# Reordering the steps of two attention mixers in a two-layer decoder trunk on one NeuronCore

## Chip, core and metric

The kernel runs on one core of a Trainium2 chip. The metric is device time in microseconds (us) of one execution. Before the change the median of three runs is 2033.67 us (2032.64 to 2034.67).

## What is computed

The input is 512 positions of width 1024, float32. Each of two layers adds half a SwiGLU feed-forward (width 2816), a mixer, and half a SwiGLU again. The reference, cut to what matters:

```python
for layer in range(2):
    x = x + 0.5 * swiglu_half(x, ffn1...)
    h = rms_norm(x, mix_norm[layer])
    if layer == 0:
        z = h @ ab_w_in
        mixed = concat([mla_mixer(z[..., :416], ...), dilated_mixer(z[..., 416:], ...)]) @ ab_w_out
    else:
        z = h @ cd_w_in
        mixed = concat([swa_mixer(z[..., :768], ...), nsa_mixer(z[..., 768:], ...)]) @ cd_w_out
    x = x + mixed
    x = x + 0.5 * swiglu_half(x, ffn2...)
```

`mla_mixer` projects to a latent, expands it to 8 heads of queries and keys, norms them, rotates a part and attends causally. `dilated_mixer` has three groups of 4 heads with bands at distances 1, 4 and 16, merged by their log-sum-exp. `swa_mixer` is banded attention with sinks (window 128, 8 query heads, 2 key heads). `nsa_mixer` adds compressed, selected and windowed attention under gates (8 query heads, 2 key heads).

## The kernel before

Every product of float32 matrices is made from three matmuls (`TERMS`): each operand is split into a high and a low float32r part (`split`, L164: ScalarE copies the high part, VectorE subtracts), and high x high, high x low and low x high are summed in PSUM. Weights stream from HBM through three `raw` buffers on SyncE's queue, and are split as they come (`weight`, L131). Activations lie transposed, 8 tiles of 128 x 512 (`xh`, `xl`).

`build` runs feed-forward, `mix0`, feed-forward, feed-forward, `mix1`, feed-forward. Each feed-forward is 1584 matmuls of 512 columns.

A mixer is a list of steps. `emit` (L111) walks a string (`ORDER0`, L42, or `ORDER1`, L47); each word names a step, and the digits are its arguments. The steps are recorded in that order, and the order sets their priority; a word with `!` is recorded with the priority of the mixer's start, so a scheduler in the build places it as early as its inputs and buffers let it. The scheduler then fixes one order for each engine, and at run time each engine takes its instructions strictly in that order, waiting at any whose input isn't there. PSUM has 8 banks by use: two for scores (`s`), two for transposes (`t`), one for an attention output (`o`), one for transposes of queries and keys (`q`), two for products (`f`).

The steps of the first mixer (`mix0`, L594):

- `a10`, `a00`, `a20`: projection of queries and keys of a dilated group (`proj`, L386: 96 matmuls of 512 columns, out `pz`), then `head_norm` (L409) on VectorE. `a01`, `a11`, `a21`: transposes of the normed result (`pt<-zqk`). `a12`, `a02`: projection of values (96 matmuls, of 512 and of 256 columns).
- `p0`, `p1`: `latent_prep` (L762) of four latent heads each: 36 matmuls (out `pq`, `pk`), squares, a chain of small VectorE operations (`rsq`, `rsqrt`), and scaling to `lq`, `lk` (L806, L807).
- `h0` to `h3`: `latent_pair` (L810), two heads of causal attention: transposes of queries and keys (`pqt<-lq`, `pqt<-lk`), scores (`s<-qt`), reduction and exponential (`scores`, L447), scaling by the row sums (`scale_rows`, L475), transposes of the weights (`pt<-e`), products with the values (`po`). `h0`, `h1` need `p0`; `h2`, `h3` need `p1`.
- `s10` and the other `s`: scores of a dilated group for a pair of heads (`s<-qkt`). `o0`, `o1`: their merge, transposes and products.

After the list, `out_projs` (L564) multiplies the features by the output weights (out `py`): 48 matmuls with the features of `h0` and `h1`, then 96 with the others.

The second mixer (`mix1`, L834) has `c`, `q0`, `q1`, `n`, `v`, `u0`, `u1`: projections of 96 matmuls of 256 columns (`part`, L839; `q` the queries of the sparse attention, `u` the banded queries, each for one key head and followed by `head_norm`); `C`: compression; `S0`, `S1`, `W0`, `W1`: splits (`stack`, L986) and transposes (`stack_t`, L993, `pqt<-qst`) of the normed queries, for the sparse (`S`) and the banded (`W`) attention; `D0`, `D1`: compressed attention; `s00`, `s01`, `s10`, `s11`: two heads each of selected and full-window attention (`selected`, L1034, scores `s<-kth,qst`); `w00` to `w11`: two heads each of banded attention (`window`, L1054).

Of the kernel before, what the change touches and what calls it, by code (L numbers as in the profile page):

```python
# [38 lines left out]
TERMS = ((0, 0), (1, 0), (0, 1))  # L39


ORDER0 = """a10 p0 a00 a20 a01 h0 !a11 a12 a02 !h1 p1 s10 h2 !s00 a21 s02 !s11 !s12 s01 h3 !o0 !o1"""  # L42

SCALE_F, SCALE_D, SCALE_T, SCALE_W = "vgvg", "gavv", "ggav", "avgv"
SQUARE = "ggva"
PARTS0 = [1, 0], [3, 4, 5, 2]
ORDER1 = """c q0 C n S0 q1 !v D0 s00 u0 !u1 W0 s01 w00 !S1 !W1 w01 !D1 s10 !w10 s11 w11"""  # L47
PARTS1 = [5, 4], [2, 6], [1, 0, 3, 7]


# [8 lines left out]
class Trunk:  # L59
# [534 lines left out]
    def mix0(self, nj):  # L594
# [29 lines left out]
        def turned(g):  # L624
# [9 lines left out]
        sc = [{}, {}]  # L634
        self.emit(ORDER0, {
            "a": lambda g, n: (queries_keys, turned, values)[n](g),
# [197 lines left out]
    def mix1(self, nj):  # L834
# [4 lines left out]
        def part(n, scaled=False):  # L839
            z = two([self.u("z", "zp") for _ in range(2)])  # L840
            self.proj(A["cd%d" % n], nat,
                      lambda i, p: nc.scalar.activation(z[i], p, AF.Copy, scale=r[:, i:i + 1] if scaled else 1.0))
            return z

        def heads(z):
            self.head_norm([t.rearrange("p (h e) -> p h e", h=4) for t in z], r=r)
            return z
# [34 lines left out]
        def kv():  # L882
# [3 lines left out]
        self.hold = None  # L886
        self.emit(ORDER1, {
            "q": lambda g: zq.update({g: heads(part((2, 6)[g]))}),
# [301 lines left out]
```

## Time and profile before

| what | value |
| --- | --- |
| runs | 2032.64, 2033.67, 2034.67 us |
| profiled execution, its own time | 2036.73 us |
| its span, first to last instruction | 2034.9 us |
| TensorE (PE) busy | 1991.1 us, 98% |
| VectorE (DVE) busy | 1012.5 us, 50% |
| ScalarE (ACT) busy | 756.0 us, 37% |
| GpSimd (POOL) busy | 159.2 us, 8% |
| mean granted TensorE clock | 0.988 of full |

Times inside the execution are microseconds from the span's start. A busy time of PE is a sum over what ran, and a matmul at a lower granted clock is longer, so PE can be busy all the time and still lose time to the clock. The first mixer lies at about 375 to 670, the second at about 1390 to 1670.

### The profile page before, as it was taken

Reading aid. Unit: us, or ns where it says so; the run is one execution under the profiler, and the core shown is the slowest. Engines: PE = TensorE matmul, PEld = TensorE weight load, DVE = VectorE, ACT = ScalarE, POOL = GpSimd, SP = SyncE. Lnnn points to the kernel's source line nnn. Section 1 sums busy time; section 2 is a strip of 40 time slices with the busy share of each in tenths; the row PEclk is TensorE's granted clock in tenths of the full one; section 3 lists DMA queues with packets and bytes.
Section 4 is the critical chain, followed back from the end, with each engine's and each line's share of the span. In section 5 each row is a group of like instructions: output and inputs, shape, how many; then the busy total and the mean of one; then the engine's idle time right before and its main releaser. Section 6 shows DMA issues by size and latency. Waiting matters only on the chain. (4 is left out here: it accounts for less than half of the span.)

```text
span 2034.9 us, 24712 instructions
## 1 busy us (share of the span) xinstructions
PE 1991.1 (98%) x9559; PEld 1639.8 (81%) x9559; DVE 1012.5 (50%) x1956; ACT 756.0 (37%) x1298; POOL 159.2 (8%) x219
## 2 busy tenths in 40 slices
PE   8999999999989999999999999999999999999999
PEld 6888888987857888888888888889976678888887
DVE  6443444474455644344454434444766666433442
ACT  4222333345546432223333223333367753322231
POOL 6000001011022100000100000011011120000000
PEclk9999999999979999999999999999999999999999
DMA  6523224431111322322332332244202032233223
GB/s 189 179 88 109 99 87 131 132 98 42 45 42 45 114 100 85 105 94 95 92 110 88 95 102 104 92 150 146 73 19 74 23 102 95 90 93 107 104 87 100
DMA packets 72853, 194.54 MB, mean 96 GB/s; under 512 B 9540, under 2 KB 16216, under 8 KB 72736
## 3 DMA queue, kind: packets, MB, share of 16 engines
q1 hardware_dynamic: 70752, 186.90, 27.9%
q0 software_dynamic: 1984, 6.06, 1.2%
q8 instruction: 75, 1.23, 0.3%
q14 instruction: 42, 0.34, 0.0%
HBM read 186.59 MB, written 12.35 MB: 98 GB/s over the span
## 5 line engine op out<-in xcount | busy, mean ns | idle before, releaser
L169 DVE TENSOR_TENSOR wlo<-raw,whi 128x1024 fp32r<-128x1024 f32 (+4 forms) x386 | 397.5, 1030 | 521.4 <-ACT whi L168 512.2
L168 ACT CAST whi<-raw 128x1024 fp32r<-128x1024 f32 (+4 forms) x386 | 345.3, 895 | 738.9 <-PE pu L162 298.9
L162 PE MATMUL pg<-xh,whi 128*128 128x512 f32 x704 | 276.1, 392 | 6.7 <-ACT xh L171 6.7
L162 PE MATMUL pg<-xl,whi 128*128 128x512 f32 x704 | 275.4, 391 | 1.5 <-DVE xl L172 1.5
L162 PE MATMUL pg<-xh,wlo 128*128 128x512 f32 x704 | 276.0, 392 | 0.0
L162 PE MATMUL pu<-xh,wlo 128*128 128x512 f32 x704 | 274.6, 390 | 0.0
L162 PE MATMUL pu<-xh,whi 128*128 128x512 f32 x704 | 274.3, 390 | 0.0
L162 PE MATMUL pu<-xl,whi 128*128 128x512 f32 x704 | 273.9, 389 | 0.0
L162 PE MATMUL py<-ah,whi 128*128 128x512 f32 x704 | 273.9, 389 | 0.0
L162 PE MATMUL py<-al,whi 128*128 128x512 f32 x704 | 273.9, 389 | 0.0
L162 PE MATMUL py<-ah,wlo 128*128 128x512 f32 x704 | 273.9, 389 | 0.0
L301 ACT ACTIVATE tg<-tg 128x512 f32<-128x512 f32 x88 | 55.6, 632 | 323.0 <-DVE tg L300 323.0
L162 PEld LDWEIGHTS pg<-xh,whi 128*128 128x128 f32 x704 | 132.7, 188 | 36.1 <-ACT xh L171 7.8
L162 PEld LDWEIGHTS pg<-xh,wlo 128*128 128x128 f32 x704 | 132.8, 189 | 34.7 <-DVE wlo L169 1.0
L162 PEld LDWEIGHTS pg<-xl,whi 128*128 128x128 f32 x704 | 132.6, 188 | 28.5 <-DVE xl L172 3.7
L162 PEld LDWEIGHTS pu<-xh,wlo 128*128 128x128 f32 x704 | 132.3, 188 | 27.6 <-issue 0.2
L162 PEld LDWEIGHTS pu<-xl,whi 128*128 128x128 f32 x704 | 132.1, 188 | 27.7 <-issue 0.2
L162 PEld LDWEIGHTS pu<-xh,whi 128*128 128x128 f32 x704 | 132.3, 188 | 27.4
L162 PEld LDWEIGHTS py<-al,whi 128*128 128x128 f32 x704 | 132.1, 188 | 27.5
L162 PEld LDWEIGHTS py<-ah,wlo 128*128 128x128 f32 x704 | 132.1, 188 | 27.4
L162 PEld LDWEIGHTS py<-ah,whi 128*128 128x128 f32 x704 | 132.1, 188 | 27.4
L300 DVE TENSOR_TENSOR tg<-pg,rb 128x512 f32<-128x512 f32 x88 | 60.8, 691 | 179.3 <-PE pg L162 179.2
(291 smaller groups left out, 2616.6 us busy)
## 6 DMA issues: line engine op xcount, KB each, us to landing
raw<-in_gu SPq DMA_DIRECT2D x174, 512.0 KB, 3.6
raw<-in_dn SPq DMA_DIRECT2D x64, 384.0 KB, 3.0
raw<-in_dn SPq DMA_DIRECT2D x64, 320.0 KB, 2.8
raw<-in_cd SPq DMA_DIRECT2D x14, 512.0 KB, 3.4
raw<-in_abqk SPq DMA_DIRECT2D x12, 512.0 KB, 3.8
xd<-x SPq DMA_DIRECT2D x16, 256.0 KB, 2.0
x<-xd SPq DMA_DIRECT2D x16, 256.0 KB, 3.3
raw<-in_abv SPq DMA_DIRECT2D x6, 512.0 KB, 3.6
```

The source lines that it names most:

```text
L162: self.nc.tensor.matmul(p, lhsT=w, rhs=x, start=n == 0, stop=n == len(terms) - 1)
L168: nc.scalar.copy(hi, src)
L169: nc.vector.tensor_tensor(lo, src, hi.bitcast(F32), OP.subtract)
L300: nc.vector.tensor_tensor(tg, ps[0], rb, OP.mult)
L301: nc.scalar.activation(tg, tg, AF.Silu)
```

## The change

Only the two strings change. The steps are the same ones, with the same instructions.

```diff
-ORDER0 = """a10 p0 a00 a20 a01 h0 !a11 a12 a02 !h1 p1 s10 h2 !s00 a21 s02 !s11 !s12 s01 h3 !o0 !o1"""
+ORDER0 = """a10 !p0 a00 !h0 !h1 !p1 a20 a01 a11 a12 a02 !h2 s10 !s00 a21 s02 !h3 !s11 !s12 s01 !o0 !o1"""
-ORDER1 = """c q0 C n S0 q1 !v D0 s00 u0 !u1 W0 s01 w00 !S1 !W1 w01 !D1 s10 !w10 s11 w11"""
+ORDER1 = """c q0 C n S0 u0 !v D0 s00 q1 W0 s01 w00 u1 !S1 w01 !D1 W1 s10 !w10 s11 w11"""
```

In the first mixer `p0` and the pairs `h0`, `h1` move up into the projections `a10` and `a00`; `p1` moves to just ahead of `a20`; `h2` moves into the projection `a12`. In the second, `u0` takes the place of `q1`, `q1` follows `s00`, and `u1` is spread between `s01` and `w00` without its `!`.

First place: PE at the start of the third latent pair, `h2` (its first instructions are the transposes `pqt` of `lq` and `lk`). Before:

```order
L456 MATMUL s_4326<-qkt 128x256 x2
L162 MATMUL py<-ol,whi 128x512
L162 MATMUL py<-oh,whi 128x512
L162 MATMUL py<-oh,wlo 128x512
L162 MATMUL py<-ol,whi 128x512
L456 MATMUL s_4327<-qkt 128x256 x2
L434 MATMUL pqt<-ident,lq 96x128 x4
L434 MATMUL pqt<-ident,lk 96x128 x4
L456 MATMUL s_4359<-qt 128x512
L456 MATMUL s_4360<-qt 128x384
```

After the change:

```order
L404 MATMUL pz<-wlo,xh 128x512
L434 MATMUL pqt<-ident,lq 96x128 x4
L404 MATMUL pz<-whi,xl 128x512
L404 MATMUL pz<-whi,xh 128x512
L404 MATMUL pz<-wlo,xh 128x512
L404 MATMUL pz<-whi,xl 128x512
L434 MATMUL pqt<-ident,lk 96x128 x4
L404 MATMUL pz<-whi,xh 128x512
L404 MATMUL pz<-wlo,xh 128x512
L404 MATMUL pz<-whi,xl 128x512
L404 MATMUL pz<-whi,xh 128x512
L456 MATMUL s_4323<-qt 128x512
```

The pair stood behind the dilated scores `s10`, right after `p1`, with no projection left; now it stands among the matmuls of `a12`, and between its first transposes and its last product there are 52 of them.

Second place: PE at the start of the first latent pair, `h0`. After the change it lies in `a00`, 33 matmuls of `a00` behind the last matmul of `p0`:

```order
L404 MATMUL pz<-whi,xl 128x512
L404 MATMUL pz<-whi,xh 128x512
L434 MATMUL pqt<-ident,lq 96x128
L404 MATMUL pz<-wlo,xh 128x512
L404 MATMUL pz<-whi,xl 128x512
L434 MATMUL pqt<-ident,lq 96x128
L404 MATMUL pz<-whi,xh 128x512
L404 MATMUL pz<-wlo,xh 128x512
L404 MATMUL pz<-whi,xl 128x512
L434 MATMUL pqt<-ident,lq 96x128
L404 MATMUL pz<-whi,xh 128x512
```

Before, the whole of `a20` and most of `a00` stood between `p0` and `h0`; now the four transposes of `lq` alternate with what is left of `a00`. From there to the last product of `h1` stand 47 matmuls of `a00`, 7 of `a20` and the 36 of `p1`.

Third place: PE in the second mixer at the first transposes of `W0` (`pqt<-identr,qst`) inside `s01`. Before:

```order
L456 MATMUL s_11944<-ktl,qst 128x256
L456 MATMUL s_11966<-kth,qst 128x512
L456 MATMUL s_11966<-ktl,qst 128x512
L434 MATMUL pqt<-identr,qst 128x128 x4
L456 MATMUL s_11967<-kth,qst 128x384
L456 MATMUL s_11967<-ktl,qst 128x384
L434 MATMUL pqt<-identr,qst 128x128 x4
L456 MATMUL s_11968<-kth,qst 128x256
```

After the change:

```order
L434 MATMUL pqt<-identr,qst 128x128 x4
L404 MATMUL pz<-wlo,xh 128x256
L404 MATMUL pz<-whi,xl 128x256
L404 MATMUL pz<-whi,xh 128x256
L404 MATMUL pz<-wlo,xh 128x256
L404 MATMUL pz<-whi,xl 128x256
L404 MATMUL pz<-whi,xh 128x256
L434 MATMUL pqt<-identr,qst 128x128 x4
L456 MATMUL s_11817<-kth,qst 128x512
L456 MATMUL s_11817<-ktl,qst 128x512
L404 MATMUL pz<-wlo,xh 128x256
L456 MATMUL s_11818<-kth,qst 128x384
```

Before, `u1` was finished by then and `s01` ran alone; now the matmuls of `u1` (`pz`) stand between the scores of `s01` and the transposes of `W0`.

On VectorE the splits that feed these transposes (`qst<-zp`, L169 in `stack`) stood behind the norm of `u0` in the middle of `s01`. Now the norm of `u0` and those four splits stand ahead of the first scores of `s00`. All DMAs are the same ones; on SyncE's queue only the two loads of `p1` (`raw<-in_qb`, `raw<-in_kvb`) move, ahead of the loads of `a20`, and loads of biases and of output weights change places by a few.

## Rows read from the trace of the kernel before

**Rows 1.** Page, busy time (part 1) and granted clock in 40 slices (part 2).

```profile
PE 1991.1 (98%) x9559; PEld 1639.8 (81%) x9559; DVE 1012.5 (50%) x1956; ACT 756.0 (37%) x1298; POOL 159.2 (8%) x219
...
PEclk9999999999979999999999999999999999999999
```

**Rows 2.** Busy time by stage: stretch, length, busy by engine, clock, DMA, GB/s.

```profile
375.00:670.00 295.00, 276.50 (x1424) 228.09 (x1423) 168.52 (x522) 149.87 (x319) 49.87 (x69) 0.95 0.21 67
...
1030.00:1390.00 360.00, 360.00 (x1587) 296.75 (x1586) 163.28 (x200) 109.04 (x137) 9.60 (x7) 1.00 0.32 107
1390.00:1670.00 280.00, 267.35 (x1785) 221.77 (x1784) 185.85 (x617) 164.64 (x424) 42.60 (x61) 0.97 0.21 67
```

**Rows 3.** Busy time by stretch inside the first mixer, same columns.

```profile
480.00:500.00 20.00, 16.23 (x87) 10.58 (x86) 8.08 (x27) 14.18 (x33) 2.52 (x4) 1.00 0.00 1
500.00:548.00 48.00, 48.00 (x276) 42.62 (x274) 18.49 (x43) 25.47 (x59) 2.54 (x4) 1.00 0.13 39
548.00:572.00 24.00, 15.24 (x49) 8.52 (x48) 15.24 (x60) 10.61 (x34) 4.29 (x6) 0.79 0.06 17
572.00:590.00 18.00, 15.34 (x84) 9.83 (x84) 6.98 (x31) 12.20 (x36) 2.38 (x4) 0.91 0.00 1
590.00:612.00 22.00, 19.71 (x93) 13.89 (x89) 15.74 (x89) 10.51 (x22) 8.26 (x8) 0.69 0.30 96
612.00:670.00 58.00, 56.97 (x361) 43.99 (x360) 34.74 (x89) 35.65 (x74) 17.32 (x30) 1.00 0.20 67
```

**Rows 4.** The same inside the second mixer.

```profile
1520.00:1540.00 20.00, 13.41 (x71) 9.59 (x70) 17.66 (x72) 16.27 (x47) 3.09 (x4) 0.83 0.06 14
...
1570.00:1610.00 40.00, 35.76 (x186) 23.88 (x185) 28.58 (x112) 28.11 (x88) 8.65 (x14) 0.87 0.12 34
```

**Rows 5.** Timeline of PE where `h2` begins: start, length, instruction, idle before and releaser.

```profile
547.76 0.40 PE L162 MATMUL pk<-wp,ltl 128*128 128x512 f32 x1
...
554.27 1.13 PE L456 MATMUL s<-qkt 64*128 64x256 f32 x4
559.10 0.31 PE L434 MATMUL pqt<-ident,lq 128*96 128x128 f32 x1 [3.71 <-DVE lq L807]
561.09 0.45 PE L434 MATMUL pqt<-ident,lq 128*96 128x128 f32 x1 [1.67 <-DVE lq L807]
```

**Rows 6.** Busy time of the ten microseconds around those transposes, columns of rows 2.

```profile
560.00:570.00 10.00, 6.79 (x16) 3.67 (x17) 3.98 (x13) 2.47 (x5) 0.75 (x2) 0.50 0.00 0
```

**Rows 7.** Timeline of DVE, the first query tile of `p1`.

```profile
558.21 0.83 DVE L807 TENSOR_TENSOR lq<-lq,mr 128x256 f32<-128x256 f32 x1
```

**Rows 8.** Timeline of PE: last matmul of `p0`, then neighbouring matmuls of `a00`.

```profile
428.55 0.40 PE L162 MATMUL pk<-wp,ltl 128*128 128x512 f32 x1
...
429.00 0.39 PE L404 MATMUL pz<-whi,xh 128*128 128x512 f32 x1
429.24 0.40 PE L404 MATMUL pz<-wlo,xh 128*128 128x512 f32 x1
```

**Rows 9.** Timeline of DVE, the first query tile of `p0`.

```profile
440.13 0.84 DVE L807 TENSOR_TENSOR lq<-lq,mr 128x256 f32<-128x256 f32 x1
```

**Rows 10.** Busy time from `h0`'s first transposes to `h1`'s last product.

```profile
480.00:528.40 48.40, 44.63 (x226) 34.37 (x224) 19.73 (x55) 30.14 (x70) 5.05 (x8) 1.00 0.10 31
```

**Rows 11.** Timeline of PE in the second mixer, first transposes of `W0` and of `S1`.

```profile
1520.63 0.39 PE L456 MATMUL s<-ktl,qst 128*128 128x512 f32 x1
1525.02 0.50 PE L434 MATMUL pqt<-identr,qst 128*128 128x128 f32 x4 [4.00 <-DVE rsm L220]
...
1534.94 0.66 PE L434 MATMUL pkt<-ident,kd 128*128 128x128 f32 x4 [2.38 <-ACT qst L998]
```

**Rows 12.** Timeline of DVE there: norm of `u0`, splits of the queries.

```profile
1517.35 1.51 DVE L427 TENSOR_TENSOR zp<-zp,hr 128x256 f32<-128x256 f32 x3
...
1520.04 2.43 DVE L169 TENSOR_TENSOR qst<-zp,qst 128x256 fp32r<-128x256 f32 x7
```

**Rows 13.** Busy time of two stretches behind those waits, columns of rows 2.

```profile
1525.90:1529.40 3.50, 3.50 (x17) 2.94 (x17) 2.73 (x16) 2.75 (x9) 0.31 (x1) 0.51 0.00 0
1536.20:1539.70 3.50, 3.50 (x12) 1.86 (x10) 1.96 (x7) 2.83 (x9) 0.00 (x0) 0.51 0.14 37
```

**Rows 14.** Waits of PE in the first mixer: in total, times, longest.

```profile
PE pqt L434 <- DVE lq L807: 6.0, 4, 3.7
PE pt L434 <- DVE e L480: 4.3, 3, 1.8
```

**Rows 15.** Timeline of PE in `h0` before: the first transposed weights.

```profile
487.44 0.33 PE L434 MATMUL pt<-ident,e 128*128 128x128 f32 x1 [1.73 <-DVE e L480]
```

## The prediction

> **What bounds the kernel now.** I read the busy times and the clock slices of the page first: PE is busy 98% of the span, no other engine over 50%, and the clock digits fall below 9 at one place [rows 1]. So time can come only from PE's idle time or from its clock. The split by stage says where: a feed-forward of 360 us has PE busy for 360.00 at clock 1.00, while the first mixer has 276.50 of 295 busy at 0.95 and the second 267.35 of 280 at 0.97 [rows 2]. The two mixers thus hold 18.5 + 12.65 = 31 us of idle PE, and the part of the clock that was missing (0.05 x 295 and 0.03 x 280, some 23 us, a bit of which lies in the idle time). About 50 us is all that an order of steps could win, and the change touches exactly these two stages.
>
> Inside the first mixer [rows 3] the idle time is in four stretches: 3.8 us at 480 to 500 (pair `h0`), 8.8 us at 548 to 572 (`s10` and the start of `h2`), 2.7 at 572 to 590 (`h2`), 2.3 at 590 to 612 (`h3` with dilated scores). Where pair `h1` runs among the projections, at 500 to 548, PE is busy for all 48.00 us at clock 1.00. That is the contrast that the argument rests on: a latent pair is a chain (transposes, copy, scores, reduction, exponential, scaling, transposes, copy, product) that leaves holes on PE, and wide projection matmuls next to it fill them. In the second mixer it is 6.6 us at 1520 to 1540 and 4.2 at 1570 to 1610 [rows 4].
>
> The list of waits names the releasers: 6.0 us of PE's idle time in the first mixer ends with `lq` from VectorE, 4.3 with scaled weights [rows 14].
>
> **The change, term by term.** No instruction is added or removed, so each term is a wait or a low clock that goes or comes.
>
> 1. *Start of `h2` (gain 11).* The last matmul of `p1` ends at 548.16; VectorE needs until 558.21 + 0.83 = 559.04 to deliver the first query tile, 10.9 us later [rows 5, 7]. PE has some 7 us of dilated scores and output products meanwhile, then idles 3.71 and 1.67 us and more. The clock falls to half: in 560 to 570 PE is busy 6.79 us at 0.50 [rows 6], work that full speed does in 3.4. Together 8.8 + 3.4 = 12.2 us. After the change `h2` stands among 52 matmuls of `a12`, and `p1` is finished a whole projection earlier, so this wait has no cause. I leave 1 us for `s10`, which stays as thin as it is.
> 2. *Body of `h2` (gain 3).* 572 to 590 has 2.7 us idle and lacks 0.09 x 18 = 1.6 us of clock. I take 3 of 4.3, as `s00` and `a21` stay outside.
> 3. *`h0` (gain 3).* Its 3.8 us of idle time at 480 to 500, such as the 1.73 us before the first transposed weights [rows 15], come where only four projection matmuls stand inside the pair. Now `h0` and `h1` share 54 of them.
> 4. *Start of `h0` (loss 3).* This is the new risk, since `p0` now has little behind which to finish. From the end of its last matmul to the first query tile it took 440.97 - 428.95 = 12.0 us [rows 8, 9], and `p1` 10.9. In the new order 33 matmuls of `a00` stand there; they start 0.235 us apart [rows 8], so 7.8 us of cover. That leaves 3.1 to 4.2. In the row of `p0` four scalings of `a10`'s norm stood ahead of the tile on VectorE; they now stand behind it, which takes about 3 us off. Further tiles come about as fast as the `a00` matmuls between the transposes run out. I take 3, near the upper of 1 and 4; the far bound is the 6.0 us of [rows 14] plus 3.4 of clock.
> 5. *`h0`, `h1`, `p1` together (loss 2.5).* VectorE now has `p1` and the norm of `a00` in the same place. In 480 to 528 it was busy 19.7 of 48.4 us [rows 10]; the tail of `p1` with `s10` took 15.24 in 548 to 572 [rows 3], and the norm comes on top, so it is close to full. Scores of `h1` stand ahead of most of it, and the projection `a20` that follows covers the rest. Bounds: 0, as at 500 to 548, and 8.8, as at 548 to 572. I take 2.5, nearer to the row with matmuls of projections in it.
> 6. *The end of the attention (loss 2).* `s10`, `s00`, `a21`, `s02`, `h3`, `s11`, `s12`, `s01` now follow each other with 21 output matmuls between them. The row for this is 590 to 612, which loses 2.3 us idle and 0.31 x 22 = 6.8 of clock. I keep that loss and add 2 for `s10` and `s00`, which lose `h2` as company; bounds a gain of 5 and a loss of 10.
>
>    Those 22 us are hardly idle and yet at 0.69, of narrow scores and transposes. [...]
> 7. *`W0` in the second mixer (gain 8.5).* PE waits 4.00 us before the first transposes of `W0` and 2.38 before those of `S1` [rows 11]. VectorE was then still scaling `u0` (1517.35) and splitting the queries (1520.04 on, 2.43 us) [rows 12]; in the new order both stand ahead of the first scores of `s00`, a whole attention pair earlier, and the matmuls of `u1` run where PE idled. Two stretches of 3.4 us at half clock follow the waits, with PE busy throughout [rows 13], which cost 1.7 each. 6.6 + 3.4 = 10; I take 8.5.
> 8. *`S1`, `D1`, `W1` (loss 2).* They move together, right ahead of `s10`. Bounds 0 and 6.6, the same wait come again for `W1`; I take 2, nearer to 0, since all of `w01`, `D1` and 28 output matmuls now stand between the last matmul of `u1` and the transposes of `W1`. 1570 to 1610 keeps its order, and I count nothing there; its 4.2 us may go either way.
>
> All other moves cost nothing. The loads hide behind the projections, where PE has no idle time at 500 to 548 [rows 3]; only the two of `p1` are moved past others, ahead of `a20`'s, and if they held those up, the first matmuls of `a20` would wait for a split. The pairs `h0` and `h1`, some 45 us of PE work, lie in front of it.
>
> First mixer: 11 + 3 + 3 - 3 - 2.5 - 2 = 9.5. Second: 8.5 - 2 = 6.5. The sum is 16 us. The profiled execution took 2036.73 us (its span 2034.9 and 1.8 around it), so it would take 2020.7; it is 3.1 above the median of the runs, 2033.67, to which my number belongs: **2017.7 us**.
>
> **The rivals.**
>
> *The tail's clock eats half of it.* The end of the attention (term 6) is about 40 us long (7 for `s10` [rows 5], 22 for 590 to 612, some 11 for `s00` and `a21`, two thirds of 572 to 590). At half clock throughout it would lose 20 us in place of the 11 that I count, with 1 or 2 us of idle time more: some 2028. For it speaks 590 to 612 at 0.69, against it 612 to 670 at 1.00.
>
> *Waits only change place.* The waits removed were backlogs of VectorE. If `h0`'s start costs the full 9.4 us (term 4), `h1` and `p1` another 5 and `W1` the 4.00 of `W0`, the losses are 9.4 + 5 + 2 + 4 = 20 in place of 9.5, and the gain is 5: 2028 to 2034, hardly to be told from no change (4 us, 0.2%, is about what a measurement can tell). For it: VectorE is busy 71 to 88% of the bad stretches of the second mixer [rows 4]. Against it: the same backlogs do no harm where projections lie beside them.
>
> *Slower: the first two pairs run thin.* In the place from `h0`'s first transposes to `h1`'s last product PE has about 45 us of work: the two pairs take 44.6 us busy less 72 matmuls of `a12` (17.0) and the transposes of `a11` (some 2.5), so 25 [rows 10]; 54 wide matmuls add 12.7 and the 36 of `p1` (384 and 512 columns) some 7. If VectorE falls behind there and PE runs as in 548 to 572, busy for 15.24 of 24 us at 0.79, those 45 us take 71, with no gain left at term 3 either: 2017.7 + 26 + 1, about 2045. It decides from the point where that stretch takes over 66 us (45 + 5 already counted + 16). Against it: the 54 wide matmuls and `p1`'s 36 are spread through it, and in 500 to 548 that was enough.
>
> *Better than forecast.* If terms 4 to 6 and 8 come to nothing, the gain is 25 us, 2008; with a better clock in the tail 2003.
>
> That the order is not really changed is excluded by the order of the instructions, which shows each move.
>
> **How the numbers follow.** Forecast, gain of 8 to 26 us: 0.62, as each removed wait has its releaser in a row and its cover in the new order. Better still: 0.06. The tail's clock, 2026 to 2030: 0.09. Waits only change place, 2030 to 2038: 0.10. Slower, from 2038 on: 0.13. Faster by over 0.2% (under 2029.6) holds the first three, nearly: 0.76. Within 0.2%: 0.11. Slower: 0.13. The range of 8 in 10 goes from 2006 to 2039: it leaves out the better end and the slow rival's core, some 0.18, and holds the bounds of terms 4 to 6.
>
> **What would show it.** In the profile after, the two transposes of `lq` with 3.71 and 1.67 us before them, and the one of `W0` with 4.00, should be gone, the mixers should be near 285 and 273 us long, and the list of waits should have `pqt` on `lq` with some 3 us, now at `h0`. A clock under 0.9 between `h0` and `h1`, or VectorE at 90% there, would make the forecast wrong; so would idle time before the transposes of `W1`, or 20 us at half clock around `h3`.

## The result, and the profile after

The changed kernel takes 2002.97 us (median of 4 runs, 2002.49 to 2004.07) against 2034.17 us (4 runs) for the old one: a ratio of 0.9847, with a 95% interval of 0.983 to 0.9864. That is 31 us faster. I had forecast 16, and 2003 lies below my range of 2006 to 2039. On another occasion (e10 below) the same kernel took 2010.43 us, ratio 0.9876 [0.9862, 0.9891], which lies inside that range; why it differs is part of the answer.

The page of the changed kernel, busy times and granted clock in 40 slices, to be set beside [rows 1]:

```profile
PE 1975.6 (99%) x9559; PEld 1628.5 (81%) x9559; DVE 1011.0 (51%) x1956; ACT 754.2 (38%) x1298; POOL 157.6 (8%) x219
...
PEclk9999999999999999999999999999999999999999
```

The slice that fell below 9 is gone. PE is also busy for 15.5 us less with the same 9559 matmuls: most of the work that ran at half clock (26.1 and 16.8 us in the two mixers) now runs at full (6.8 and 0 us at half are left). By stage and by stretch, after the change (stretch, length, then busy time of PE, PE's weight loads, VectorE, ScalarE, GpSimd, then granted clock, DMA share, GB/s):

```profile
375.00:653.00 278.00, 270.01 (x1425) 222.01 (x1424) 169.31 (x522) 149.62 (x319) 48.97 (x69) 0.99 0.22 71
...
1373.00:1637.00 264.00, 258.93 (x1785) 217.56 (x1784) 184.34 (x618) 163.04 (x424) 42.02 (x61) 1.00 0.22 71
```

```profile
431.00:440.20 9.20, 7.83 (x35) 5.90 (x35) 9.13 (x37) 3.81 (x7) 2.52 (x4) 1.00 0.12 31
440.20:488.40 48.20, 46.99 (x227) 32.44 (x227) 33.08 (x92) 32.76 (x78) 8.57 (x13) 0.96 0.16 55
...
522.90:549.00 26.10, 26.10 (x129) 21.93 (x129) 8.81 (x25) 15.03 (x35) 2.52 (x4) 1.00 0.05 17
...
560.50:574.00 13.50, 12.74 (x77) 8.78 (x76) 6.68 (x35) 11.60 (x41) 0.00 (x0) 1.00 0.16 39
574.00:601.00 27.00, 23.79 (x131) 15.63 (x128) 21.36 (x104) 15.04 (x36) 9.61 (x11) 0.94 0.25 83
```

```profile
1490.00:1512.00 22.00, 21.40 (x162) 18.64 (x161) 18.34 (x74) 18.77 (x55) 3.94 (x6) 1.00 0.09 23
1512.00:1528.00 16.00, 15.85 (x115) 12.02 (x114) 8.34 (x32) 10.38 (x33) 3.62 (x6) 1.00 0.12 38
1528.00:1545.00 17.00, 14.80 (x97) 11.13 (x97) 15.87 (x59) 14.25 (x43) 1.19 (x2) 1.00 0.34 110
...
1560.00:1610.00 50.00, 49.06 (x299) 33.30 (x295) 33.14 (x126) 37.94 (x121) 9.56 (x16) 1.00 0.14 43
```

Against [rows 2], the first mixer fell from 295 to 278 us and the second from 280 to 264. Idle time of PE in the two went from 18.5 + 12.65 to 8.0 + 5.1, 18 us; the rest, 15 us, is less busy time, beside 41 us less at half clock (table below). In the pieces:

- `h2` lies in 522.9 to 549: PE busy for 26.10 of 26.10 us at 1.00, where [rows 5, 6] had waits of 3.71 and 1.67 and half clock.
- `h0`, `h1` and `p1` lie in 440.2 to 488.4. Nothing is lost there apart from the waits at `h0`'s start and 3.4 us at half clock behind them.
- The end of the attention, `s10` to `h3`, lies in 560.5 to 601. It loses 0.8 + 3.2 us idle, at 1.00 and 0.94, where the row of 590 to 612 in [rows 3] stood at 0.69.
- `W0` lies in 1490 to 1512, with 0.6 us idle, and the wait of 4.00 us [rows 11] is gone; 1560 to 1610 holds `s10`, `w10` and half of `s11`, with 0.94 us idle at 1.00. The nearest stretch in [rows 4], 1570 to 1610, which also holds the end of `w01`, had 4.24 us idle at 0.87.

The one new wait that I had named is there. PE at the start of `h0` (start, length, instruction, idle before and releaser):

```profile
440.17 0.31 PE L434 MATMUL pqt<-ident,lq 128*96 128x128 f32 x1 [1.37 <-DVE lq L807]
...
442.16 0.32 PE L434 MATMUL pqt<-ident,lq 128*96 128x128 f32 x1 [1.21 <-DVE lq L807]
```

### The profile page after: what moved, and what is told of

It is laid out like the page before. It is cut to its first block, busy times and chain, and to the rows that moved or that the text cites. A ratio compares the mean times of both kernels' runs of the same rounds, so it can differ in the third digit from the quotient of the medians.

```text
span 2001.3 us, 24703 instructions
## 1 busy us (share of the span) xinstructions
PE 1975.6 (99%) x9559; PEld 1628.5 (81%) x9559; DVE 1011.0 (51%) x1956; ACT 754.2 (38%) x1298; POOL 157.6 (8%) x219
## 4 chain that ended last, share of the span: by engine, by line
PE 95%; DVE 2%; ACT 1%; issue 1%; DMA 0%; POOL 0%; SPq 0%; DVEq 0%; ACTq 0%; POOLq 0%
PE py L162 27%; PE pg L162 24%; PE pu L162 24%; PE pz L404 10%; PE s L456 3%; PE po L497 2%; PE pt L434 2%; PE pqt L434 1%; ACT e L451 1%; PE pq L162 0%; PE ph L931 0%; DMA x<-in_xT 0%; ACT th L443 0%; DVE e L450 0%; PE pk L162 0%
## 5 line engine op out<-in xcount | busy, mean ns | idle before, releaser
L169 DVE TENSOR_TENSOR wlo<-raw,whi 128x1024 fp32r<-128x1024 f32 (+4 forms) x386 | 397.3, 1029 | 518.4 <-ACT whi L168 512.5
```

Source lines behind the costliest of these rows:

```text
L169: nc.vector.tensor_tensor(lo, src, hi.bitcast(F32), OP.subtract)
```

## The experiments

Twelve kernels; in eleven of them nothing but the two order strings is edited, and e10 is the changed kernel once more. In the table a mixer's length goes from the end of the last feed-forward matmul before it to the start of the first one behind it, "idle" is PE's idle time in it and "half" the time for which the granted clock was 0.50 of full there, all three from the one profiled execution; the median and the ratio to the old kernel are of all timed runs.

| kernel | first mixer: us, idle, half | second mixer: us, idle, half | median us | ratio, 95% interval |
| --- | --- | --- | --- | --- |
| old | 295.2, 18.5, 30.7 | 279.9, 12.6, 17.1 | 2034.2 | 1 |
| changed | 278.0, 8.0, 6.8 | 263.8, 5.1, 0 | 2003.0 | 0.9847 [0.983, 0.9864] |
| e1 | 276.5, 8.2, 3.4 | 276.7, 12.6, 10.2 | 2017.6 | 0.9924 [0.9897, 0.9951] |
| e2 | 295.1, 18.5, 30.7 | 265.6, 5.3, 3.4 | 2021.8 | 0.9938 [0.9919, 0.9957] |
| e3 | 286.6, 10.2, 23.9 | 271.1, 8.3, 6.8 | 2016.5 | 0.991 [0.9888, 0.9932] |
| e4 | 296.3, 21.0, 30.7 | 272.0, 7.1, 10.2 | 2028.2 | 0.997 [0.9959, 0.998] |
| e5 | 277.5, 8.1, 6.8 | 268.6, 7.1, 3.4 | 2006.6 | 0.9862 [0.9847, 0.9876] |
| e6 | 276.6, 9.8, 10.2 | 263.9, 5.0, 0 | 2003.3 | 0.9845 [0.9831, 0.986] |
| e7 | 292.9, 11.2, 34.1 | 264.0, 5.2, 0 | 2010.5 | 0.9885 [0.9855, 0.9914] |
| e8 | 288.4, 12.2, 27.3 | 265.6, 5.2, 3.4 | 2010.1 | 0.9875 [0.9858, 0.9891] |
| e9 | 277.3, 8.1, 6.8 | 264.1, 5.2, 0 | 2003.7 | 0.9848 [0.9834, 0.9861] |
| e10 | 279.6, 8.1, 10.2 | 263.9, 5.1, 0 | 2010.4 | 0.9876 [0.9862, 0.9891] |
| e11 | 283.8, 12.6, 17.1 | 280.0, 12.6, 17.1 | 2024.1 | 0.9936 [0.9917, 0.9954] |
| e12 | 276.5, 8.9, 0 | 265.5, 5.0, 3.4 | 2003.6 | 0.9842 [0.9828, 0.9857] |

### e1 and e2: one mixer at a time

e1 is the old kernel with the new `ORDER0`, e2 the old kernel with the new `ORDER1`.

> First mixer in the new order, second in the old one. Theory (the two mixers are separate, each gain is made in its own stage): the first mixer takes 278 us as in the changed kernel, the second 280 as before, the total is 17.3 us below before, about 2017. Rival (part of the second mixer's gain is carried over from the first, through transfers or buffers): the second mixer takes less than 276 us and the total is under 2013.

> First mixer in the old order, second in the new one. Theory (separate stages): first mixer 295 us, second 264, total 16 us below before, about 2018. Rival (carried over): the second mixer takes over 268 us and the total is over 2022.

The theory held for the stages. Each mixer has the idle time of its own order whatever the other does, and the two gains, 0.76% and 0.62%, make up most of the 1.5% together; e2's total of 2021.8 us is 4 above the one expected and just under the rival's 2022. One thing was not expected: the second mixer in its old order took 276.7 us in e1 and 280 in the old kernel and in e11, with the same 12.6 us idle and 10.2 in place of 17 us at half clock. With the same order and the same idle time, 6.8 us less at half clock made it 3.2 us shorter.

### e3, e4, e5: which move mended `W0` and `w01`

e3 against the old kernel:

```diff
-a10 p0 a00 a20 a01 h0 !a11 a12 a02 !h1 p1 s10 h2 !s00 a21 s02 !s11 !s12 s01 h3 !o0 !o1
+a10 p0 a00 a20 a01 h0 !a11 !p1 a12 a02 !h1 !h2 s10 !s00 a21 s02 !s11 !s12 s01 h3 !o0 !o1
-c q0 C n S0 q1 !v D0 s00 u0 !u1 W0 s01 w00 !S1 !W1 w01 !D1 s10 !w10 s11 w11
+c q0 C n S0 u0 !v D0 s00 q1 !u1 W0 s01 w00 !S1 !W1 w01 !D1 s10 !w10 s11 w11
```

> Old orders with one move in each: in the first mixer p1 goes ahead of a12 and h2 ahead of s10 (h0 and the end of the attention keep their places, h3 stays last), in the second u0 and q1 change places. First mixer, theory (each hole has its own releaser): only the losses at the start and in the body of h2 go, 9 to 14 us, and the loss of 9 us where h3 and the dilated scores run stays: 281 to 286 us, with some 10 us at half clock there. Rival (the thin end was a consequence of h2's late start): the clock stays at 1.00 there as well and the mixer takes 277 to 280. Second mixer, theory: the wait of 4.00 us before the transposes of W0 goes, the one of 1.85 before those of w01 stays: 269 to 273 us. Rival (w01 waits because of the backlog that begins at W0): both go, 264 to 267 us. Total by the theory about 2013 to 2017, by both rivals 2002 to 2007.

e4 against the old kernel, first mixer unchanged:

```diff
-c q0 C n S0 q1 !v D0 s00 u0 !u1 W0 s01 w00 !S1 !W1 w01 !D1 s10 !w10 s11 w11
+c q0 C n S0 q1 !v D0 s00 u0 W0 s01 w00 u1 !S1 !W1 w01 !D1 s10 !w10 s11 w11
```

> Old orders, but u1 of the second mixer goes from before W0 to behind w00, as in the changed kernel. Theory (w01 waits for its exponential because few wide matmuls stand beside it): with the 48 matmuls of u1 beside it the hole of 1.85 us before its transposes and the half clock behind go (4 to 6 us of gain), while the wait before W0 stays and loses the matmuls of u1 as cover (0 to 5 us lost): second mixer 275 to 281 us. Rival (w01 waits because of the backlog that begins at W0): the hole of w01 is still there, over 1 us, and the mixer takes 280 to 286. First mixer 295 in both.

e5 against the changed kernel:

```diff
-c q0 C n S0 u0 !v D0 s00 q1 W0 s01 w00 u1 !S1 w01 !D1 W1 s10 !w10 s11 w11
+c q0 C n S0 u0 !v D0 s00 q1 W0 s01 w00 !u1 !S1 w01 !D1 W1 s10 !w10 s11 w11
```

> The changed kernel with one mark more: u1 of the second mixer, in its new place behind w00, is given the early priority again, so that 72 of its matmuls stand in one block ahead of the transposes of W0, as in the old kernel, while u0 stays early. Theory (the wait before W0 went because u1's matmuls are now spread between the scores of s01): the holes before the transposes of W0 (3 to 4 us) and S1 (about 2 us) are back, the second mixer takes 270 to 276 us in place of 264, the total is 2009 to 2016. Rival (my step on W0: it went because u0 and the queries come a pair earlier): no hole over 1 us there, second mixer 263 to 267, total 2002 to 2006. The first mixer is unchanged, 276 to 278.

Neither of my explanations of `W0` was the right one. In e3 `u0` is early, and the wait before `W0`'s query transposes is still there (3.42 us); the mixer's 271 us lie where the theory put them, but because the wait in `w01` went, which the theory had as staying. In e4 `u0` is as late as before, and the wait is gone, so that 272 us lie below the 275 that the theory gave. In e5 `u1` runs as one block again, and the wait does not come back; taken alone e5 would speak for my step on `W0`, though its mixer is 1.6 us above the rival's range, but e3 and e4 speak against it. So with `u1` recorded ahead of `W0` there is a wait, whether `u0` is late (4.00 us, the old kernel) or early (3.42, e3), and with `u1` behind it there is none, whether `u0` is late (e4) or early (e5 and the changed kernel). The reason shows on VectorE. `W0` first transposes its keys (`pkt<-ident,kd`) into the one PSUM buffer for queries and keys; its query transposes (`pqt`) need that buffer, which is free once ScalarE and VectorE have read the keys, VectorE last (`ktl<-pkt`, L172). In e3, at that place, PE, then VectorE, then PE again:

```profile
1501.24 0.60 PE L434 MATMUL pkt<-ident,kd 128*128 128x128 f32 x4
```

```profile
1515.35 0.74 DVE L172 SCALAR_TENSOR_TENSOR ktl<-pkt,sgain,kth 128x512 fp32r<-128x512 f32 x1
```

```profile
1516.24 0.72 PE L434 MATMUL pqt<-identr,qst 128*128 128x128 f32 x4 [3.42 <-DVE rsm L220]
```

The keys lie transposed at 1501.84, and VectorE comes to them 13.5 us later; the query transposes follow 0.15 us after the read ends. The releaser that the trace names, `rsm` (L220), is the instruction right behind the read on VectorE and no input of the transposes. The old kernel, PE and then VectorE:

```profile
1509.44 0.60 PE L434 MATMUL pkt<-ident,kd 128*128 128x128 f32 x4
```

```profile
1524.12 0.75 DVE L172 SCALAR_TENSOR_TENSOR ktl<-pkt,sgain,kth 128x512 fp32r<-128x512 f32 x1
```

There too the transposes of [rows 11], at 1525.02, start 0.15 us after the read ends. The same pair of lines in the changed kernel, PE and then VectorE:

```profile
1489.93 0.60 PE L434 MATMUL pkt<-ident,kd 128*128 128x128 f32 x4
```

```profile
1493.12 0.74 DVE L172 SCALAR_TENSOR_TENSOR ktl<-pkt,sgain,kth 128x512 fp32r<-128x512 f32 x1
```

From the start of the key transposes to the start of this read it took 14.7 us in the old kernel, 14.1 in e3, 6.7 in e4 (1509.36 to 1516.08), 3.2 in e5 and in the changed kernel. So VectorE's queue decides: with `u1` recorded first, the read stands behind the norm of the projection before it (`u0` in the old kernel, `q1` in e3), the query splits that follow this norm and the squares of `u1`. Spreading `u1`'s matmuls is a second, smaller gain: e5, where they are a block, takes 268.6 us against 263.8, with 2 us more idle, most of it in `w01` and `s10`.

The transposes of `w01`, with 2.4 us idle before and among them in the old kernel (1.85 of it in one wait), have none in e3 and e4 and 1.2 us in e5. In e3 seven output matmuls and two scores stand between those transposes, in the old kernel all of them ahead. Which move puts them there was not tried one by one.

In the first mixer of e3, `h2`'s waits are down to 0.88 and 0.45 us as the theory had it, while the end of the attention kept its loss: 17 us at half clock where some 10 were expected, 286.6 us, just above the range.

The first mixer of e4 is the old one, with the same instructions in the same order on every engine, and yet it was idle for 21.0 us in place of 18.5. The difference lies at the end of the attention. The last 424 matmuls of the mixer, in the old kernel and in e4:

```profile
593.60:670.20 76.60, 73.69 (x426) 55.75 (x426) 48.83 (x160) 44.64 (x93) 25.02 (x38) 0.91 0.24 78
```

```profile
596.00:672.30 76.30, 70.39 (x426) 52.83 (x426) 49.26 (x160) 44.75 (x93) 25.01 (x38) 0.96 0.25 78
```

In the old kernel 13.7 us of this stretch were at half clock, in e4 6.8. The time is the same: where the clock was higher PE waited longer, 5.9 us in place of 2.9, most of it for VectorE's part of the dilated softmax (`sp`, L553).

### e6 and e8: where `h3` stands

e6, against the changed kernel:

```diff
-a10 !p0 a00 !h0 !h1 !p1 a20 a01 a11 a12 a02 !h2 s10 !s00 a21 s02 !h3 !s11 !s12 s01 !o0 !o1
+a10 !p0 a00 !h0 !h1 !p1 a20 a01 a11 a12 a02 !h2 s10 !s00 a21 s02 !s11 !s12 s01 h3 !o0 !o1
```

> The changed kernel with h3 of the first mixer behind s11, s12 and s01 again. Theory (the end of the attention gained because h3's chain now has those dilated scores beside it): 1.5 to 3 us more idle time and 7 to 17 us at half clock between 575 and 610, first mixer 281 to 287 us, total 2006 to 2012. Rival (it gained because the stretch now follows two projections and has wide output matmuls in it): 276 to 279, total 2002 to 2005. Second mixer 264 to 266.

e8, against the changed kernel:

```diff
-a10 !p0 a00 !h0 !h1 !p1 a20 a01 a11 a12 a02 !h2 s10 !s00 a21 s02 !h3 !s11 !s12 s01 !o0 !o1
+a10 !p0 a00 !h0 !h1 !p1 a20 a01 a11 a12 !h2 a02 !h3 s10 !s00 a21 s02 !s11 !s12 s01 !o0 !o1
```

> The changed kernel with h2 and h3 together among the matmuls of a12 and the start of a02, so that the end of the attention holds dilated scores and output matmuls alone. Theory (a chain leaves no hole where projections lie beside it): the idle time of 3 to 4 us between 571 and 601 and its half clock go, nothing new comes, first mixer 272 to 275 us, total 1997 to 2000. Rival (VectorE, with both pairs and the rest of p1 in one place, falls behind): 2 us or more of idle time among a12's matmuls, first mixer 277 to 282, total 2002 to 2008.

e6 went by the rival: 1.8 us more idle, no longer time. `h3`'s place among the last scores is not what the end gained by. It also shows the clock at work: from the transposes of `a21` to the end of the mixer it has the same 504 matmuls as e3, with the steps in the same order, and took 90.5 us with 6.8 of them at half clock, where e3 took 94.6 with 17.

e8 went against both. PE is idle for only 0.28 us from 510 to 590, around `a12`, so `h2` and `h3` together are no burden to VectorE; but the end became worse without `h3`. Waits of PE in e8 from 560 to 640 (us in total, times, longest), and PE's busy time there:

```profile
PE py L162 <- DVE x L583: 3.6, 2, 3.5
PE s L456 <- DVE sp L553: 2.9, 2, 1.7
PE pst L695 <- issue: 1.4, 1, 1.4
```

```profile
597.00:618.00 21.00, 14.40 (x42) 10.60 (x41) 13.94 (x49) 5.84 (x11) 6.05 (x6) 0.51 0.10 29
```

The dilated scores now wait for VectorE's part of the dilated softmax (2.9 us), and output matmuls for its additions to `x` (L583, 3.6 us): 6.6 of 21 us are idle, at half clock. `h3` had been their cover, as much as they were its.

### e7: `h0` without its priority

```diff
-a10 !p0 a00 !h0 !h1 !p1 a20 a01 a11 a12 a02 !h2 s10 !s00 a21 s02 !h3 !s11 !s12 s01 !o0 !o1
+a10 !p0 a00 h0 !h1 !p1 a20 a01 a11 a12 a02 !h2 s10 !s00 a21 s02 !h3 !s11 !s12 s01 !o0 !o1
```

> The changed kernel without the early priority of h0: 80 matmuls of a00 in place of 33 stand between p0 and h0, but only 24 matmuls of a20 inside the two pairs in place of 54. Theory (VectorE's 12 us behind p0 are the only reason of the wait at h0's start, and pairs with p1's matmuls beside them are covered): the holes of 1.37 and 1.21 us and the half clock go, first mixer 273 to 277 us, total 1998 to 2002. Rival (pairs with few projection matmuls run thin, the slower case of the forecast): 3 to 9 us of idle time between the first transposes of h0 and the last product of h1, the clock falls there, first mixer 279 to 290, total 2004 to 2016.

The rival held, with a first mixer of 292.9 us even longer than its 290. The wait at `h0`'s start is gone, but with 24 in place of 54 projection matmuls inside, the two pairs have waits of 2.43, 0.67, 0.89 and 0.96 us; idle time of the mixer is up by 3.2 us. This is the slower case of my forecast, at a fraction of its price. Of the 14.9 us by which the first mixer is longer than in the profile of the changed kernel, 8.5 lie in the end of the attention, which has the same matmuls in the same order. PE there in the changed kernel:

```profile
575.72 0.64 PE L434 MATMUL pqt<-ident,lk 128*96 128x128 f32 x4 [0.77 <-ACT qt L445]
577.03 1.77 PE L456 MATMUL s<-qt 96*128 96x512 f32 x4 [0.67 <-ACT qt L443]
...
580.97 0.64 PE L434 MATMUL pqt<-ident,lk 128*96 128x128 f32 x4 [0.98 <-ACT qt L445]
582.26 0.73 PE L162 MATMUL py<-oh,whi 128*128 128x512 f32 x1 [0.65 <-DVE x L583]
```

And in e7:

```profile
582.95 0.64 PE L434 MATMUL pqt<-ident,lk 128*96 128x128 f32 x4 [0.77 <-ACT qt L445]
584.26 1.77 PE L456 MATMUL s<-qt 96*128 96x512 f32 x4 [0.67 <-ACT qt L443]
...
588.20 0.64 PE L434 MATMUL pqt<-ident,lk 128*96 128x128 f32 x4 [0.98 <-ACT qt L445]
589.71 0.50 PE L162 MATMUL py<-oh,whi 128*128 128x512 f32 x1 [0.86 <-DVE x L583]
```

The first three waits are the same, and the fourth is longer by 0.21 us. What follows is not the same: busy time and clock behind them, in the changed kernel and in e7:

```profile
582.40:585.80 3.40, 3.40 (x6) 1.56 (x7) 2.23 (x5) 0.34 (x1) 1.13 (x2) 0.50 0.95 307
```

```profile
591.00:615.00 24.00, 24.00 (x86) 17.45 (x86) 12.96 (x71) 8.66 (x20) 6.40 (x8) 0.50 0.12 41
```

The changed kernel has half clock for 3.4 us, e7 for 24 with PE busy throughout. e1 and e5, with the same matmuls in the same order, have none at all; the fourth wait is 0.85 us long in e1, so its length does not decide. From the transposes of `a21` to the end of the mixer, the same 504 matmuls in e1, the changed kernel and e7:

```profile
561.46:651.96 90.50, 84.87 (x507) 61.59 (x506) 58.08 (x212) 56.06 (x134) 25.82 (x38) 1.00 0.24 72
```

```profile
561.33:653.07 91.74, 86.33 (x507) 62.25 (x506) 58.66 (x212) 56.12 (x134) 25.42 (x38) 0.98 0.23 71
```

```profile
568.56:668.81 100.25, 94.88 (x507) 69.16 (x506) 58.34 (x212) 56.72 (x134) 25.46 (x38) 0.88 0.21 65
```

Here the low clock is paid: 24 us of it made the stretch 9.8 us longer than in e1, at the same idle time.

### e9 and e10: is the clock of that end fixed by the order?

e9, against the changed kernel (`a02` is 96 matmuls of 256 columns); e10 is the changed kernel with no edit:

```diff
-a10 !p0 a00 !h0 !h1 !p1 a20 a01 a11 a12 a02 !h2 s10 !s00 a21 s02 !h3 !s11 !s12 s01 !o0 !o1
+a10 !p0 a00 !h0 !h1 !p1 a20 a01 a11 a12 !h2 s10 !s00 a21 s02 a02 !h3 !s11 !s12 s01 !o0 !o1
```

> The changed kernel with the 96 wide matmuls of a02 not ahead of the end of the attention but inside it, behind s02 and ahead of h3 (they and the output matmuls then stand in small groups between the dilated scores, the transposes of a21 and the chain of h3). Theory (the end is thin because few wide matmuls stand in it, and a thin stretch may fall to half clock in one execution and not in the next): idle time of the first mixer 8 us down to 4 or 6, at most 3.4 us at half clock behind 560, first mixer 273 to 276 us, total 1998 to 2001, and the single times lie within 4 us of each other. Rival (the end is bound by its own chain through VectorE, ScalarE and GpSimd, and wide matmuls only move the holes behind them): idle time stays at 7 to 10 us, total 2002 to 2010.

> The changed kernel once more, nothing edited, to see what its clock does in other executions. Theory (the clock of the end of the attention is not fixed by the order of the instructions: the same holes were followed by 0, 3.4 and 23.9 us at half clock in three kernels): some of its times lie 3 us or more above the 2003 of before, up to 2012. Rival (with this order the clock holds): all times within 2 us of 2003.

e10 by the theory: its four runs took 2005.62, 2008.46, 2012.39 and 2013.24 us at mean granted clocks of 0.997, 0.995, 0.993 and 0.992; the four of the first measurement had 0.998 or 0.999. So the changed kernel lies anywhere from 2002.5 to 2013.2, in the order of its clock. The old kernel, timed beside e10, took 2035.2 us against 2034.2 the first time, so the occasion was not slower for every kernel. It follows that medians between 2003 and 2013 do not rank e5 to e8 and e12 against the changed kernel, which was not timed beside them; what these runs show is the idle time and the waits in their profiles. e9 went half by each side: the idle time did not fall (8.1 us; a wait of 2.01 us for VectorE now stands before an output matmul behind the dilated scores), but its five runs took 2002.28 to 2005.46 at 0.996 to 0.998. Beside e10 on the same chip it is faster, with intervals that do not meet; beside the first measurement it is the same. That its clock is steadier rests on five runs against eight and is no more than likely.

### e11: one step moved in the old order

```diff
-a10 p0 a00 a20 a01 h0 !a11 a12 a02 !h1 p1 s10 h2 !s00 a21 s02 !s11 !s12 s01 h3 !o0 !o1
+a10 p0 a00 a20 a01 h0 !a11 a12 !h1 p1 s10 h2 !s00 a21 s02 a02 !s11 !s12 s01 h3 !o0 !o1
```

> The old orders with one step of the first mixer moved: a02 from ahead of h1 to behind s02, so that its 96 wide matmuls stand between p1 and h2 and among h2's first transposes. Theory (a latent pair costs what its cover leaves open): the waits of 3.71 and 1.67 us for the first tiles of p1 and the half clock behind them go, 8 to 13 us of gain, first mixer 282 to 287 us, second 280, total 2021 to 2026. Rival (the pair waits for VectorE whatever stands beside it, and the hole moves to h1 or to the body of h2): first mixer 290 us or more, total 2029 or more.

As the theory had it: of the 3.71 and 1.67 us at `h2`'s start 1.08 is left, with 3.4 in place of 10.2 us at half clock behind it; the mixer falls by 11.4 us, the total to 2024. The wait needs matmuls beside it; here they are `a02`'s and in the changed kernel `a12`'s.

### e12: `p0` first

e12 is e9 with `!p0` ahead of `a10`.

> As e9, and p0 ahead of a10, so that the norm of a10 no longer stands between p0 and the first query tiles on VectorE. Theory (the start of h0 waits because VectorE does a10's norm, some 3 us, and a weight split in the 12 us behind p0): the holes of 1.37 and 1.21 us shrink to under 1 us together, the half clock behind them goes, first mixer 273 to 275 us, total 1999 to 2002. Rival (p0 then waits itself, for its latents, or h0 and h1 lose the cover of a00): 2 us or more of idle time between 398 and 490 as in e9, first mixer 277 or more, total 2003 to 2008.

This went by the rival: 3.2 us idle between 398 and 490, a total of 2003.6, though the mixer is not longer. The waits at `h0`'s start fell from 2.58 to 1.35 us, but not because `a10`'s norm is out of the way. The last matmul of `p0` and the first query tile in the changed kernel, PE and then VectorE:

```profile
430.82 0.40 PE L162 MATMUL pk<-wp,ltl 128*128 128x512 f32 x1
```

```profile
439.28 0.83 DVE L807 TENSOR_TENSOR lq<-lq,mr 128x256 f32<-128x256 f32 x1
```

And in e12:

```profile
410.01 0.40 PE L162 MATMUL pk<-wp,ltl 128*128 128x512 f32 x1
```

```profile
418.37 0.84 DVE L807 TENSOR_TENSOR lq<-lq,mr 128x256 f32<-128x256 f32 x1
```

From the end of the one to the end of the other VectorE takes 8.9 us in the changed kernel and 8.8 in e12, so `a10`'s norm is not what the first tile waits for. PE only waits elsewhere: 0.63 us before `p0`, 0.23 and 0.27 among the projection matmuls behind it. Idle time is 8.9 us against 8.1 and the time that of e9, so there is nothing to gain in it. No version clearly beat the changed kernel's best measurement; e9 and e12 reach it.

## Why the prediction was wrong

The direction, the places and most waits were right, and the sum was half of what came. Terms in its own order; a gain is what the stretch lost before less what it loses now.

- *Terms 1 and 2* (forecast 14): right, and a little small. The stretch of `h2` loses nothing now, so all 16.5 us came. e11 shows the mechanism by itself.
- *Term 3* (3): right, 3.8 us.
- *Term 4* (loss 3): about right. 2.58 us of waits on `lq`, and 0.04 x 48.2 = 1.9 by the clock, 4.5 in all.
- *Term 5* (loss 2.5): it did not come. VectorE was busy for 33 of 48 us there, not close to full. e7 shows that this holds only with enough projection matmuls inside.
- *Term 6* (loss 2 on top of the 9.1 of 590 to 612): **the first large step that failed**, "I keep that loss and add 2". The end lost 4.0 us idle and 0.06 x 27 = 1.6 by the clock, 5.6 in place of 11.1. The idle part was right (2.3 and most of the 2 on top); the 6.8 of clock were mis-sized, because they were carried over from another order as if they came with the steps. In the new order the idle time is about 4 us in every profile and the low clock behind it is 0, 3.4 or 24 us (e1, changed, e7), so the loss goes from 4 to about 14 and my 11 lies inside; the rival on the tail's clock is in part what e7's profile shows. In the old order the loss was firm: e4, with 0.86 in place of 0.69 between 590 and 612, was idle for 6.1 us there in place of 2.3, 9.1 us lost both times. Why the new order does not lose it no run isolates; e6 shows only that it isn't the place of `h3`.
- *Term 7* (8.5): the size was right (6.6 us of waits and 3.4 by the clock, less 0.75 that is left), the reason half wrong. It was VectorE's backlog, but on the key tile, and what moved it was `u1` behind `W0`. `u0` ahead of `s00`, the move that I named, left 3.42 us (e3).
- *Term 8* (loss 2): its first half was right, 2.5 us idle in 1528 to 1560. Its second half is **the largest miss**: "1570 to 1610 keeps its order, and I count nothing there". The stretch lost 4.24 us idle and some 5 by the clock, and 1560 to 1610 loses 0.94 now: 8.5 us that the sum didn't have. PE in the old kernel there:

```profile
1572.27 0.33 PE L434 MATMUL pt<-ident,e 128*128 128x128 f32 x1 [1.85 <-ACT e L478]
...
1602.92 0.66 PE L434 MATMUL pt<-ident,e 128*128 128x128 f32 x4 [1.35 <-DVE e L480]
```

The first of these waits belongs to `w01`, which had moved: `u1` now stands ahead of it, and `W1` behind it. I had read the stretch by its time and not by its step. The second belongs to `s10`, which did keep its place. It is still there in e5, where only `u1`'s mark differs from the changed kernel, so in the new order the spread of `u1`'s matmuls removes it; by what path isn't shown.

The first mixer adds up to 16.5 + 3.8 - 4.5 + 3.5 = 19.3 against 17.2 measured, the second to 9.3 - 2.5 + 8.5 = 15.3 against 16.1. Part of the first is luck that no term has: 3.4 us at half clock near 396, before any of the moved steps, are in the profiles of the old kernel, e5 and e10, and not in that of the changed kernel. Against this, the busy time of the first mixer fell by only 6.7 us, though 26.1 us of work ran at half clock before and 6.8 after; half of the difference would be 9.7. The second's fell by 8.5 for 16.8, as half gives. The 3 us that are missing in the first are not explained.

The measured time is that of my case "better than forecast", 2008 or 2003 with a better clock, which I gave 0.06; but its condition, that terms 4 to 6 and 8 come to nothing, was not met, so that the number agrees is luck. That the result lies outside my range is in part chance too: the four times of e10, at a lower clock, have a median of 2010.4, which lies inside it. Its profile has the same 8.1 and 5.1 us idle, so terms 6 and 8 would be as wrong. The waits only changing place, and the pairs running thin, did not come in this order; e8 and e7 have them on a small scale, after a word or two moved.

## What to carry to other kernels

Read each idle stretch by the step that its first late instruction belongs to, and ask whether that step moves, before writing that a stretch stays as it is. Where a wait ends on a buffer, follow the last engine that reads the buffer and see what is recorded ahead of that read on its queue: here one word's place in the list was worth a wait of 4 us. Take the large waits as what an order fixes (the two mixers of the changed kernel were idle for 8.0 and 5.1 us in one profile, 8.1 and 5.1 in the other), and low clock behind them as a loss that may or may not come: price it from nothing (e1) to nearly half of the thin stretch (9.8 us for 24 at half clock in e7), expect less where PE would otherwise wait (0.3 us for 6.8 at half clock, the old kernel against e4), and time such a kernel on more than one occasion.

## What was not expected of the hardware

The same matmuls, behind nearly the same waits (0.65 to 0.98 us in the changed kernel and e7), ran at a granted clock of 1.00 throughout in e1's profile (561 to 652), with 3.4 us at 0.50 in that of the changed kernel (582.4 to 585.8) and 24 us at 0.50 in that of e7 (591 to 615), PE busy all the while at 0.50. For the changed kernel there is a spread of 2002.5 to 2013.2 us in eight runs, and the time follows the mean granted clock (2002.49 us at 0.999, 2013.24 at 0.992); e7's four runs, all on one chip, took 2005.5 to 2018.9 (at 0.999 and 0.992). In one respect the profiles agree: in the first mixer of the changed order half clock begins at the same few places of the program, near 396, 443 and 583, and it is which of them fall that differs (the last two in the changed kernel, the second in e1, the first two in e5, all three in e10). What decides which of them fall, no run here shows.

What low clock costs depends on what PE would do otherwise. In the end of the new order 24 us of it cost 9.8 us (e7 against e1); in the end of the old order 6.8 us more of it cost 0.3 us (the old kernel against e4), as PE waits for VectorE there at the higher clock (5.9 us idle in place of 2.9).

In e8 the stretch at 0.51, 597 to 618, begins with dilated scores and output matmuls and no transposes, as `h3` had left it; the output matmuls of 602 to 610 take 0.63 us each, where one at 593.83 took 0.40. So transposes are not needed for the clock to fall there. In the old kernel 590 to 612 and 612 to 670, which the prediction compares, hold transposes in the same share, 20 of 93 and 80 of 361 matmuls, at 0.69 and at 1.00.
